# Unnormed rows from transposed loads, with the reciprocal rms applied where projections are evacuated

## The chip, the core and the metric

The kernel runs on one core of a Trainium2 chip. Its engines work side by side, each in the order of its own queue: TensorE (PE, with its weight loads as PEld), VectorE (DVE), ScalarE (ACT), GpSimd (POOL), and SyncE (SP), which here issues every DMA. The metric is device time in microseconds, the median of the runs.

## What is computed

One layer of a streaming encoder: y = x + W_out [A | B | M]. Every row of x is divided by its rms and multiplied by a gain g, and one input projection of the result is cut into columns for three groups of heads: A, differential attention (4 heads, with q and k normed per head); B, an mLSTM (4 heads); M, cross-attention into 256 memory tokens, whose rows are normed and projected in the same way. There are 1024 prompt tokens and 8 x 16 decode tokens, which have caches of 1024 keys.

```python
def rms_norm(x, g):
    xf = x.astype(F32)
    y = xf * lax.rsqrt(jnp.mean(xf * xf, axis=-1, keepdims=True) + EPS)
    return (y * g.astype(F32)).astype(x.dtype)
...
h = rms_norm(x, g_norm)
z = jnp.einsum('bsd,de->bse', h, w_in)
qa, ka, va, ga, qb, kb, vb, ob, ib, fb, gb, qm, gm = split_cols(z)
qa = rms_norm(qa.reshape(B, S, H_A, 2, DK_A), g_qa)
```

The reciprocal rms is one number for a row. It can be taken out of the sum over d: z is that number times the projection of the unnormed row. In q and k, which are normed again, it cancels except in the eps.

## The kernel before

The tokens are 9 tiles of 128 rows: the decode tile DEC first, then the prompt tiles from last to first (`order`). A product of fp32 precision is made of three: each operand is split into a hi part (fp32r) and a lo remainder, and hi x hi, hi x lo and lo x hi are summed in PSUM. With 8 steps over d a projection of a tile onto 512 columns has 24 products of 128x512 (`project`, L247). `weights` (L213) loads 8 tiles of a weight (`wraw`), makes the hi part `wh` on ACT (L231, the gain as scale) and the lo part `wl` on DVE (L238), or on POOL for the steps that a table names (L235 and L236; in phase A0 step 5).

The phases follow each other: A0 to A3 (the four heads of A; A0 also makes the transposed tiles `hth` and `htl` that all phases use), with the memory tiles between A0 and A1; then G (gates), M, B0 and B1 (pairs of heads of B, and beside them the decode attention over the caches, which loads 32 MB of keys and values), and the output projection O0 and O1. In phase A0 `norm_x` prepares a tile ahead of the one that is projected:

- The first tile (`norm_first`, L264) and the second (`norm_T` with `split_T`, L298 and L193) are squared on ACT for their sum, rooted on POOL (`root`, L133, as a power), scaled on DVE, transposed by PE (L279, L200), and split: the hi part copied on ACT, the lo part subtracted on DVE.
- Tiles 2 to 8 are loaded twice, as rows and, from a transposed input `xT`, already transposed. The rows serve only for the sum of squares (L287). PE then broadcasts the reciprocal rms over the partitions (a product of `xss` with the identity, L292), DVE scales `xT` by it (L294), ACT copies the hi part (L295), and DVE and POOL subtract a half each (L296).
- The two memory tiles are loaded as rows, scaled and transposed like the second tile, 8 transposes each.

Behind a projection come its stages. `a_post` squares q and k (ACT, L341), sums (DVE, L343), roots (POOL, L133, tile `asm`), multiplies (DVE, L345 and the gains in L395), transposes by PE (L404, tile `and__`) and splits again. The gate (`agt`) and the values (`avg`) are read from the same bank of PSUM, and the bank is free when they are. `PHASES` names the banks that z may use: in A0 two ("z").

Nothing orders the engines by hand: a scheduler lays out every engine's queue from the code and a few priorities. A change in one phase can therefore move instructions in all later ones.

Of the kernel before, what the change touches and what calls it, by code (L numbers as in the profile page):

```python
# [53 lines left out]
# steps of the decode attention after each tile of the head pairs of B  # L54
# [4 lines left out]
def hymba_step(ctx: ExitStack, tc: tile.TileContext, a: dict, o: dict):  # L59
# [61 lines left out]
    # ------------------------------------------------------------------ constants  # L121
# [39 lines left out]
    def small_loads():  # L161
# [3 lines left out]
        # carried here: the roots of n, the halves of silu and sigmoid (written with tanh), and, in  # L165
        # the gain of q, 8 * 0.125 / slope of the next head
# [20 lines left out]
        # sgn[r] = 1 on the rows of map 0, -lam on those of map 1, rows (h, m, q)  # L187
# [6 lines left out]
    def split_T(src, hi, lo, n):  # L194
        """transpose n [128,128] column blocks of src, split into hi and lo [128, n, 128]"""
# [7 lines left out]
    # the tensor engine's clock rises while the first loads run  # L203
# [9 lines left out]
    def weights(w, c0, n, gain=None, spare=()):  # L213
        """columns c0 to c0 + n of a [1024, .] weight, as hi and lo k-tiles; gain scales its rows.
        spare: (pool, tag, bufs) for raw tiles, where there is room"""
        wraw = (wpool, "wraw", 4)
        with ahead(phase.weights):
            src = [wraw] * 4 + [(p_, g_, b_) for p_, g_, b_ in spare for _ in range(b_)]
            ws = []
            for k in range(NK):  # L220
                p_, g_, b_ = src[k] if k < len(src) else wraw
                raw = p_.tile([P, 512], F32, tag=g_, name="wraw", bufs=b_)
                if spare and k == 6:
                    load_x(1)
                SY.dma_start(out=raw[:, 0:n], in_=w[k * P:(k + 1) * P, c0:c0 + n])
# [38 lines left out]
    def norm_first(xt, xp, hi, lo):  # L264
        ss = xp.tile([P, 3], F32, tag="xss0", name="xss0")
        for c in range(2):
            cs = slice(c * 512, c * 512 + 512)
            S.activation(flat(hi)[:, cs], xt[:, cs], AF.Square, accum_out=ss[:, c:c + 1])
        V.scalar_tensor_tensor(ss[:, 0:1], ss[:, 0:1], D * EPS, ss[:, 1:2], ALU.add, ALU.add)
        root(ss[:, 2:3], ss[:, 0:1])  # L270
        for c in range(4):
            cs = slice(c * 256, c * 256 + 256)
            V.tensor_scalar(xt[:, cs], xt[:, cs], ss[:, 2:3], math.sqrt(D), ALU.mult, ALU.mult)
            if c % 2:
                ks = slice(c * 2 - 2, c * 2 + 2)
                tv = bank("tp").rearrange("p (a b) -> p a b", b=P)
                for j in range(4):
                    x0 = (c - 1) * 256 + j * P
                    PE.transpose(tv[:, j, :], xt[:, x0:x0 + P], ident)  # L279
                S.copy(hi[:, ks], tv)  # L280
                V.tensor_tensor(lo[:, ks], tv, f(hi[:, ks]), ALU.subtract)  # L281

    def norm_T(xt, xp, hi, lo, xT=None):
        """rms-normed rows (gain not yet applied), transposed and split"""
        ss = xp.tile([P, 2], F32, tag="xss", name="xss", bufs=2)
        with ahead(50 if phase is PHASES["A0"] else 0):
            S.activation(hi.rearrange("p k d -> p (k d)"), xt, AF.Square, accum_out=ss[:, 0:1])  # L287
        rsqrt(ss[:, 1:2], ss[:, 0:1], D)
        if xT is not None:
            rb = bank("tp")[:, 0:P]  # L290
            mm(rb, ss[:, 1:2].broadcast_to([P, P]), ident)
            for c in range(0, NK, 4):  # L292
                cs = slice(c, c + 4)
# [389 lines left out]
    xts, xTs = {}, {}  # L683

    def load_x(i):
        if i < NT:
            xts[i] = shp.tile([P, D], F32, tag="usx", name="xt", bufs=4)
            if i == 0:
                for c in range(2):
# [617 lines left out]
```

## Time and profile before

| what | value |
| --- | --- |
| time, median of 3 runs | 783.51 us (783.5 to 788.57) |
| profiled execution, first to last instruction | 774.3 us |
| PE busy | 738.2 us (95%), 4976 products and transposes |
| DVE busy | 473.7 us (61%) |
| ACT busy | 333.4 us (43%) |
| POOL busy | 237.4 us (31%) |
| DMA | 106.19 MB, 44.2% of 16 engines' span |

The profile is of one execution. Its span runs from the first to the last instruction; of its time outside of the span only the difference to the runs is known, 9.2 us to the median. A busy share is a mean over the phases, so it is read together with the windows and with what each engine waited for. Products are pipelined and their ends are modelled, so the distance from one start to the next tells more than a duration.

### The profile page before, as it was taken

To read this page: it belongs to the slowest core of one execution; us is meant where nothing else is said; L and a number is where in the kernel's file an instruction comes from. 1 tells how busy PE (TensorE), PEld (TensorE's weight loads), DVE (VectorE), ACT (ScalarE), POOL (GpSimd) and SP (SyncE) were. 2 spreads that over 40 slices of the span, in tenths; PEclk is the share of its full clock that TensorE was granted. 3 is DMA by queue.
4 is the path that set the end of the run, shared out by engine and by line. 5 is a ranking of instruction groups with operands and counts; after the bars stand their busy time and mean duration, and the time that the engine had idled before them with its cause. 6 is when DMAs were issued, how large, how long until landed. Compare 5 with 4: busy or idle time off the path is not lost.

```text
span 774.3 us, 14523 instructions
## 1 busy us (share of the span) xinstructions
PE 738.2 (95%) x4976; PEld 599.9 (77%) x4976; DVE 473.7 (61%) x1466; ACT 333.4 (43%) x976; POOL 237.4 (31%) x332
## 2 busy tenths in 40 slices
PE   7998999999999999999999999899979997799998
PEld 6776788878888888998878776577747775578887
DVE  6788886677787778677575835347335347644111
ACT  6566634564664466555356532234223334200200
POOL 6653441323223223336313502111012036221500
PEclk9999999999999999999999999999989999999999
DMA  8733430151014112324002407979994728874422
GB/s 310 287 107 109 149 89 22 41 157 45 25 49 124 46 35 70 106 76 124 25 15 46 123 14 251 200 276 327 348 207 157 286 42 299 194 260 124 142 83 95
DMA packets 84387, 106.19 MB, mean 137 GB/s; under 512 B 16054, under 2 KB 52698, under 8 KB 84314
## 3 DMA queue, kind: packets, MB, share of 16 engines
q1 hardware_dynamic: 84314, 105.28, 44.2%
q8 instruction: 39, 0.64, 0.3%
q14 instruction: 34, 0.28, 0.1%
HBM read 86.01 MB, written 19.23 MB: 136 GB/s over the span
## 4 chain that ended last, share of the span: by engine, by line
PE 75%; DMA 9%; DVE 9%; issue 2%; ACT 2%; POOL 2%; SPq 0%; POOLq 0%; DVEq 0%; ACTq 0%
PE ps_z L95 39%; PE ps_y L95 15%; PE ps_s L95 9%; PE ps_av L95 5%; DMA kc<-in_kT_dram 4%; PE ps_tp L459 2%; DVE wl L238 2%; DMA mkc<-in_mkT_dram 1%; DMA wraw<-in_w_in_dram 1%; DMA bgt<-gated 1%; PE ps_tp L200 1%; PE ps_tp L867 1%; PE ps_tp L404 1%; DVE xT L294 1%; POOL asm L133 1%
## 5 line engine op out<-in xcount | busy, mean ns | idle before, releaser
L95 PE MATMUL ps_z<-wh,htl 128*128 128x512 f32 (+2 forms) x552 | 214.8, 391 | 0.1
L95 PE MATMUL ps_z<-wh,hth 128*128 128x512 f32 (+2 forms) x552 | 200.2, 394 | 4.4 <-ACT hth L280 2.1
L95 PE MATMUL ps_z<-wl,hth 128*128 128x512 f32 (+2 forms) x552 | 192.1, 387 | 0.0
L95 PEld LDWEIGHTS ps_z<-wh,hth 128*128 128x128 f32 x552 | 103.6, 190 | 25.5 <-ACT hth L280 2.4
L95 PEld LDWEIGHTS ps_z<-wh,htl 128*128 128x128 f32 x552 | 104.7, 190 | 18.9 <-DVE htl L281 0.8
L95 PEld LDWEIGHTS ps_z<-wl,hth 128*128 128x128 f32 x552 | 103.1, 189 | 18.6 <-issue 1.2
L95 PE MATMUL ps_y<-wh,htl 128*128 128x512 f32 (+2 forms) x176 | 65.6, 374 | 0.0
L95 PE MATMUL ps_y<-wh,hth 128*128 128x512 f32 (+2 forms) x176 | 62.9, 378 | 0.3 <-ACT oa L892 0.3
L133 POOL TENSOR_TENSOR asm<-asm,nhalf 128x4 f32<-128x4 f32 x36 | 39.6, 1100 | 74.4 <-DVE asm L137 58.8
L443 ACT ACTIVATE usx<-usx,usm 128x1024 f32<-128x1024 f32 (+7 forms) x64 | 49.7, 778 | 29.0 <-DVE usm L437 26.5
L95 PE MATMUL ps_y<-wl,hth 128*128 128x512 f32 (+2 forms) x176 | 61.3, 378 | 0.0
L238 DVE SCALAR_TENSOR_TENSOR wl<-wraw,gnm,wh 128x512 fp32r<-128x512 f32 (+1 forms) x62 | 47.0, 783 | 4.6 <-ACT wh L231 3.2
L231 ACT ACTIVATE wh<-wraw,gnm 128x512 fp32r<-128x512 f32 (+1 forms) x56 | 38.0, 706 | 18.2 <-DMA wraw<-in_w_in_dram 15.7
L95 PE MATMUL ps_s<-aqk 128*128 128x256 f32 (+1 forms) x160 | 42.0, 288 | 0.9 <-ACT aqk L412 0.9
L437 DVE CUSTOM_DVE_ANT_0 usx<-ps_s,tab 128x512 f32<-128x512 f32 (+3 forms) x64 | 37.0, 587 | 8.9 <-PE ps_s L95 7.5
L133 POOL TENSOR_TENSOR usm<-usm,nhalf 128x1 f32<-128x1 f32 x32 | 19.6, 612 | 72.3 <-DVE usm L467 67.9
L95 PE MATMUL ps_s<-akl,aqk 128*128 128x256 f32 (+1 forms) x160 | 41.0, 283 | 0.0
L95 PE MATMUL ps_av<-avg,wth 128*128 128x128 f32 x288 | 38.7, 276 | 0.2 <-DVE uot L469 0.2
L95 PEld LDWEIGHTS ps_av<-avg,wth 128*128 128x128 f32 x288 | 36.9, 191 | 2.5 <-ACT wth L460 0.6
L95 PEld LDWEIGHTS ps_y<-wh,hth 128*128 128x128 f32 x176 | 32.8, 188 | 5.8 <-ACT oa L892 0.6
L95 PEld LDWEIGHTS ps_y<-wl,hth 128*128 128x128 f32 x176 | 32.9, 188 | 5.5 <-DVE wl L238 0.3
L95 PEld LDWEIGHTS ps_y<-wh,htl 128*128 128x128 f32 x176 | 33.1, 188 | 5.0
(443 smaller groups left out, 1376.7 us busy)
## 6 DMA issues: line engine op xcount, KB each, us to landing
kc<-in_kT_dram SPq DMA_DIRECT2D x32, 512.0 KB, 8.9
vc<-in_cache_attn_v_dram SPq DMA_DIRECT2D x32, 512.0 KB, 6.8
wraw<-in_w_in_dram SPq DMA_DIRECT2D x56, 256.0 KB, 3.0
omx<-mixd SPq DMA_DIRECT2D x9, 512.0 KB, 4.1
out_dram<-oxt SPq DMA_DIRECT2D x17, 256.0 KB, 4.3
xt<-in_x_prompt_dram SPq DMA_DIRECT2D x8, 512.0 KB, 7.7
wraw<-in_w_out_dram SPq DMA_DIRECT2D x16, 256.0 KB, 4.2
oxt<-in_x_prompt_dram SPq DMA_DIRECT2D x16, 256.0 KB, 3.4
```

The source lines that it names most:

```text
L95: PE.matmul(out, lhsT, rhs, start=start, stop=stop)
L133: G.tensor_tensor(dst, ss, nhalf[:, 0:ss.shape[1]], ALU.pow)
L200: PE.transpose(tv[:, i, :], src[:, (c + i) * P:(c + i + 1) * P], ident)
L231: S.activation(wh[:, 0:n], raw[:, 0:n], AF.Copy, scale=g_)
L238: V.scalar_tensor_tensor(wl[:, 0:n], raw[:, 0:n], g_, f(wh[:, 0:n]), ALU.mult, ALU.subtract)
L294: V.scalar_tensor_tensor(xT[:, cs], xT[:, cs], math.sqrt(D), rep(rb, 4), ALU.mult, ALU.mult)
L404: PE.transpose(tp[:, i], flat(nd[:, 2 * i:2 * i + 2]), ident)
L437: V.tensor_tensor_reduce(s_[:, c * 512:c * 512 + w], sp[:, 0:w], tab[:, tx:tx + w], -slope, BIG if c == 0 else sm[:, m:m + 1], ALU.add, AL ...
L443: S.activation(s_[:, 0:nk], s_[:, 0:nk], AF.Exp, bias=last, scale=-1.0, accum_out=sm[:, 4 + m:5 + m])
L459: PE.transpose(tp[:, i], sx[0][:, (c + i) * P:(c + i + 1) * P], ident)
L867: PE.transpose(tp[0:pn, c - c0, :], se[:, c * P:c * P + pn], ident)
```

## The change

- x enters the projections unnormed. All nine tiles come from `xT`, the first in four pieces; `split_x` copies the hi part on ACT and subtracts the lo part, alternately on DVE and POOL. `norm_first`, `norm_T`, their transposes, scalings and broadcasts are gone. The memory has a transposed input too (`memT`).
- Rows are still loaded, for `row_stats`: the sum of squares (ACT), then mean plus eps and 64 eps times that (two DVE instructions of one column), the root (POOL), and the root's half and eighth (two POOL instructions of one column). They are kept in `rs`, one column for a tile.
- At every evacuation the reciprocal rms stands in: as the scale of a copy or a tanh instead of a constant or none; as a factor of an instruction that was there; or, in the gates of the decode tile and in phase G, as an added POOL multiplication. The eps of the second norms are scaled to match.
- In A0 z may use three banks ("zzy"). The loads are reordered: rows of the first tile after three weights, xT of the second and third tile before weight 6. `load_x(3)` is reached twice, from the prologue and from `norm_x(1)`.

```diff
-    "A0": Phase(300, 0, 0, 0, 4, "z", "SS", (5,), "S"),
+    "A0": Phase(300, 0, 0, 0, 4, "zzy", "SS", (5,), "S"),
...
-    def rsqrt(dst, ss, n):
-        V.tensor_scalar(ss, ss, n * EPS, None, ALU.add)
+    def rsqrt(dst, ss, n, t=None):
+        V.tensor_scalar(ss, ss, n * EPS if t is None else rsc(3, t), None, ALU.add)
         root(dst, ss)
+    def rsc(i, t):
+        return rs[:, i, t:t + 1]
...
+                if spare and k == 3:
+                    load_rows(0)
                 if spare and k == 6:
                     load_x(1)
+                    load_x(2)
...
+    def row_stats(rows, t, xp):
+        ss = xp.tile([P, 2], F32, tag="xss", name="xss", bufs=2)
+        for i, x in enumerate(rows):
+            S.activation(x, x, AF.Square, accum_out=ss[:, i:i + 1])
+        if len(rows) > 1:
+            V.tensor_tensor(ss[:, 0:1], ss[:, 0:1], ss[:, 1:2], ALU.add)
+        V.tensor_scalar(rsc(4, t), ss[:, 0:1], 1.0 / D, EPS, ALU.mult, ALU.add)
+        V.tensor_scalar(rsc(3, t), rsc(4, t), 64.0 * EPS, None, ALU.mult)
+        root(rsc(0, t), rsc(4, t))
+        G.tensor_scalar(rsc(1, t), rsc(0, t), 0.5, None, ALU.mult)
+        G.tensor_scalar(rsc(2, t), rsc(0, t), 0.125, None, ALU.mult)
+
+    def split_x(xT, hi, lo, n=2):
+        for i in range(n):
+            ks = slice(i * NK // n, (i + 1) * NK // n)
+            S.copy(hi[:, ks], xT[:, ks])
+            (V, G)[i % 2].tensor_tensor(lo[:, ks], xT[:, ks], f(hi[:, ks]), ALU.subtract)
...
-        S.activation(gt, z[:, 384:512], AF.Tanh, scale=0.5)
+        S.activation(gt, z[:, 384:512], AF.Tanh, scale=rsc(1, t))
...
+        if t == DEC:
+            G.tensor_scalar(gt, gt, rsc(0, t), None, ALU.mult)
...
-        S.copy(vg[:, j], z[:, 256:384])
+        S.activation(vg[:, j], z[:, 256:384], AF.Copy, scale=rsc(0, t))
...
+            t = order[i]
+            split_x(xTs.pop(i), hth[t], htl[t], 4 if i == 0 else 2)
+            load_x(i + 4 if i % 2 == 0 else i + 2)
...
-            norm_T(flat(mxt), ap, *mhl[t])
+            split_x(mxt, *mhl[t])
             if t == 0:
                 load_mem(1)
+            mem_stats(t)
...
             small_loads()
+            load_x(3)
             with ahead(200):
                 norm_x(0)
+            row_stats([xts.pop(0)], order[0], ap)
         for i, t in enumerate(order):
             if h == 0:
                 norm_x(i + 1)
+                if i:
+                    row_stats([xts.pop(i)], t, ap)
+                load_rows(i + 1)
...
             th4 = heads(th, 4)
+            G.tensor_scalar(th, th, rsc(0, t), None, ALU.mult)
             G.tensor_tensor(th4, th4, rep(gmh, 4), ALU.mult)
```

The scheduler's order shows three places. The first is PE's queue at the end of the first tile's products. Before, `hth_127` is the decode tile and `hth_126` the second one:

```order
L95 MATMUL ps_z<-wh,hth_127 128x512
L95 MATMUL ps_z<-wl,hth_127 128x512
L95 MATMUL ps_z<-wh,htl_136 128x512
L200 MATMUL ps_tp<-ident,xt 128x128 x8
L95 MATMUL ps_z<-wh,hth_126 128x512 x8
L95 MATMUL ps_tp<-ident,xss 128x128
```

In the change `hth_128` is the decode tile, `hth_127` and `hth_126` the second and third:

```order
L95 MATMUL ps_z<-wh,hth_128 128x512
L95 MATMUL ps_z<-wh,hth_127 128x512 x6
L95 MATMUL ps_y<-wh,hth_126 128x512 x6
L95 MATMUL ps_z<-wl,hth_128 128x512
L95 MATMUL ps_z<-wh,htl_137 128x512
L95 MATMUL ps_z<-wh,hth_128 128x512
L95 MATMUL ps_z<-wh,hth_127 128x512
L95 MATMUL ps_y<-wh,hth_126 128x512
```

The first tile is no longer finished before the second begins: after the hi product of step 5 come six hi products of each of the next two tiles, and only then the product with the lo part of step 5 (`wl`). The transposes are gone.

The second place is POOL's queue at the same time. Before:

```order
L133 TENSOR_TENSOR xss_231<-xss_231,nhalf 128x1
L387 MEMSET akl 64x256
L388 MEMSET akl 64x256
L235 TENSOR_SCALAR wraw<-wraw,gnm 128x512
L387 MEMSET akl 64x256
L388 MEMSET akl 64x256
L236 TENSOR_TENSOR wl<-wraw,wh 128x512
```

And in the change, where L245 and L246 are the weight's lines and L293 is the lo half of `split_x`:

```order
L133 TENSOR_TENSOR rs<-rs,nhalf 128x1
L285 TENSOR_SCALAR rs<-rs 128x1
L286 TENSOR_SCALAR rs<-rs 128x1
L245 TENSOR_SCALAR wraw<-wraw,gnm 128x512
L384 MEMSET akl 64x256
L385 MEMSET akl 64x256
L293 TENSOR_TENSOR htl_136<-xT,hth_127 128x512
L246 TENSOR_TENSOR wl<-wraw,wh 128x512
```

The weight's lo part, the product's operand of step 5, now stands behind the row statistics of the first tile and behind a lo half of the second.

The third place is PE's queue around the transposes of q and k (L404 before, L401 in the change) of the second tile, `and__427` before and `and__406` in the change. Before, with `hth_125` the third tile and `hth_124` the fourth:

```order
L95 MATMUL ps_z<-wl,hth_125 128x512
L404 MATMUL ps_tp<-ident,and__427 128x128 x2
L95 MATMUL ps_tp<-ident,xss 128x128
L95 MATMUL ps_z<-wh,hth_124 128x512 x8
L95 MATMUL ps_z<-wh,htl_133 128x512
```

In the change `hth_125` is the fourth tile:

```order
L95 MATMUL ps_z<-wh,htl_134 128x512
L401 MATMUL ps_tp<-ident,and__406 128x128 x2
L95 MATMUL ps_z<-wl,hth_125 128x512
L95 MATMUL ps_z<-wh,htl_134 128x512
L95 MATMUL ps_z<-wl,hth_125 128x512
L95 MATMUL ps_z<-wh,hth_124 128x512 x8
```

The transposes moved from the end of the next tile's products into those of the tile after it, and no broadcast of `xss` stands between them and the products that follow.

## Rows read from the trace of the kernel before

**Rows 1.** The page's part 1: busy us (share of the span), instructions.
```profile
PE 738.2 (95%) x4976; PEld 599.9 (77%) x4976; DVE 473.7 (61%) x1466; ACT 333.4 (43%) x976; POOL 237.4 (31%) x332
```

**Rows 2.** Windows: busy us (instructions) by engine; PE clock, DMA share, GB/s.
```profile
40.00:60.00 20.00, 17.27 (x81) 13.61 (x80) 16.77 (x39) 11.81 (x32) 10.81 (x12) 1.00 0.36 104
...
100.00:120.00 20.00, 20.00 (x106) 16.98 (x105) 15.94 (x50) 8.67 (x25) 6.04 (x10) 1.00 0.22 64
```

**Rows 3.** Timeline, PE, 0-20 us: start, duration, line, tiles, count, [idle <- releaser].
```profile
2.29 5.33 PE L95 MATMUL ps_tp<-ident 128*128 128x128 f32 x24 [2.29 <-POOL ident masks.py:199]
...
10.73 0.80 PE L95 MATMUL ps_z<-wh,hth 128*128 128x512 f32 x1 [2.13 <-ACT hth L280]
...
15.20 0.40 PE L95 MATMUL ps_z<-wh,htl 128*128 128x512 f32 x1
...
18.17 1.03 PE L200 MATMUL ps_tp<-ident,xt 128*128 128x128 f32 x8
19.50 0.73 PE L95 MATMUL ps_z<-wh,hth 128*128 128x512 f32 x2 [0.29 <-ACT hth L78]
```

**Rows 4.** Waits of PE, 10 to 95 us: total us, times, longest.
```profile
PE ps_tp L404 <- DVE and__706 L395: 1.3, 1, 1.3
PE ps_z L95 <- ACT mht L78: 1.1, 1, 1.1
PE ps_s L95 <- ACT aqk L412: 0.9, 1, 0.9
...
PE ps_tp L200 <- DVE mht L192: 0.5, 1, 0.5
```

**Rows 5.** Timeline of tiles of A0, several engines.
```profile
36.89 0.42 DVE L395 TENSOR_TENSOR and__496<-asq,vecs 128x256 f32<-128x256 f32 x1
...
50.04 1.28 POOL L296 TENSOR_TENSOR htl<-xT,hth 128x512 fp32r<-128x512 f32 x1
50.05 1.55 DVE L395 TENSOR_TENSOR and__636<-asq,vecs 128x256 f32<-128x256 f32 x1
...
51.75 0.41 PE L404 MATMUL ps_tp<-ident,and__636 128*128 128x128 f32 x2 [0.71 <-DVE and__636 L395]
51.99 0.39 PE L95 MATMUL ps_tp<-ident,xss 128*128 128x128 f32 x2
52.14 2.10 PE L95 MATMUL ps_z<-wh,hth 128*128 128x512 f32 x8
```

**Rows 6.** Timeline of PE: first products of A0's fourth tile; A0's end.
```profile
32.56 2.10 PE L95 MATMUL ps_z<-wh,hth 128*128 128x512 f32 x8
...
71.14 0.38 PE L404 MATMUL ps_tp<-ident,and__829 128*128 128x128 f32 x2
```

**Rows 7.** By line, 10-100 us: count | busy us, mean ns | idle.
```profile
L133 POOL TENSOR_TENSOR asm<-asm,nhalf 128x4 f32<-128x4 f32 x9 | 11.1, 1231 | 14.0 <-DVE xss L137 8.8 <-DVE asm L137 5.0
...
L294 DVE SCALAR_TENSOR_TENSOR xT<-xT,ps_tp 128x512 f32<-128x512 f32 x14 | 9.4, 684 | 2.6 <-PE ps_tp L95 2.5
L296 POOL TENSOR_TENSOR htl<-xT,hth 128x512 fp32r<-128x512 f32 x7 | 9.0, 1284 | 0.0
...
L133 POOL TENSOR_TENSOR xss<-xss,nhalf 128x1 f32<-128x1 f32 x10 | 6.0, 600 | 1.8 <-DVE xss L137 1.8
```

**Rows 8.** Timeline of ACT and POOL at the start: the weights' split.
```profile
6.02 4.18 ACT L231 ACTIVATE wh<-wraw,gnm 128x512 fp32r<-128x512 f32 x6 [1.09 <-DMA wraw<-in_w_in_dram]
...
10.38 2.40 POOL L235 TENSOR_SCALAR wraw<-wraw,gnm 128x512 f32<-128x512 f32 x1 [2.94 <-ACT wh L231]
...
13.48 1.29 POOL L236 TENSOR_TENSOR wl<-wraw,wh 128x512 fp32r<-128x512 f32 x1
```

**Rows 9.** DMA rate, 0 to 100 us in 40 slices of 2.5 us.
```profile
GB/s 75 277 353 368 410 419 339 262 409 413 396 319 52 159 340 55 203 36 92 170 28 209 61 35 44 0 79 0 157 277 269 265 242 7 105 0 190 234 100 208
```

**Rows 10.** PE's waits, whole span; view of tile th (min/median/max ns).
```profile
PE ps_s L95 <- DMA kc<-in_kT_dram: 7.0, 3, 3.2
...
L791 POOL TENSOR_TENSOR th<-th,vecs x9: 733/746/763, 314.8 to 352.6; 128x256 f32<-128x256 f32 x9
```

More of the change, by code (lines that the diff above doesn't have):

```diff
@@ L151, in hymba_step @@
     gif = cpool.tile([P, 2, NT, 4], F32, name="gif")
+    rs = cpool.tile([P, 5, NT + 2], F32, name="rs")
     aN, gwN, wsN, emN = (nat[:, i] for i in range(4))
@@ L262, in project @@
         return z
[L264 to L281, printed above, removed]
@@ L283, in norm_T @@
-    def norm_T(xt, xp, hi, lo, xT=None):
-        ss = xp.tile([P, 2], F32, tag="xss", name="xss", bufs=2)
[L286 to L293, printed above, removed]
-                V.scalar_tensor_tensor(xT[:, cs], xT[:, cs], math.sqrt(D), rep(rb, 4), ALU.mult, ALU.mult)
-                S.copy(hi[:, cs], xT[:, cs])
-                (V, G)[c // 4].tensor_tensor(lo[:, cs], xT[:, cs], f(hi[:, cs]), ALU.subtract)
-            return
-        V.tensor_scalar(xt, xt, ss[:, 1:2], math.sqrt(D), ALU.mult, ALU.mult)
-        split_T(xt, hi, lo, NK)
+    def row_stats(rows, t, xp):
+        ss = xp.tile([P, 2], F32, tag="xss", name="xss", bufs=2)
+        for i, x in enumerate(rows):
[7 more added lines that the diff above has]
+        G.tensor_scalar(rsc(2, t), rsc(0, t), 0.125, None, ALU.mult)
@@ L355, in a_post_dec @@
     def a_post_dec(h, z):
-        sq = a_norm(z)
+        sq = a_norm(z, DEC)
         vo = ap.tile([P, P], F32, tag="pp", name="avd", bufs=4)
-        S.copy(vo, z[:, 256:384])
+        S.activation(vo, z[:, 256:384], AF.Copy, scale=rsc(0, DEC))
         hc = slice(h * P, (h + 1) * P)
@@ L466, in a_unit @@
         S.activation(ot, av, AF.Square, accum_out=sm[:, 9:10])
[L467 removed]
+        V.scalar_tensor_tensor(sm[:, 9:10], sm[:, 9:10], sm[:, 6:7], rsc(4, t), ALU.add, ALU.mult)
         root(sm[:, 10:11], sm[:, 9:10])
@@ L590, in mem_q @@
         V.tensor_reduce(sm[:, 0], sq, AX.X, ALU.add)
-        rsqrt(sm[:, 2], sm[:, 0], 64)
-        S.activation(gt, z[:, 256:512], AF.Tanh, scale=0.5)
+        rsqrt(sm[:, 2], sm[:, 0], 64, t)
+        S.activation(gt, z[:, 256:512], AF.Tanh, scale=rsc(1, t))
         V.scalar_tensor_tensor(gt, gt, 1.0, z[:, 256:512], ALU.add, ALU.mult)
@@ L686, in load_x, with load_rows @@
         if i < NT:
-            xts[i] = shp.tile([P, D], F32, tag="usx", name="xt", bufs=4)
-            if i == 0:
-                for c in range(2):
-                    cs = slice(c * 512, c * 512 + 512)
-                    SY.dma_start(out=xts[i][:, cs], in_=xsrc(order[i], cs))
-                return
+            if i % 2:
+                xTs[i] = shp.tile([P, NK, P], F32, tag="usx", name="xT", bufs=4)
+            else:
+                xTs[i] = mp.tile([P, NK, P], F32, tag="mk", name="xT", bufs=2)
+            n = 4 if i == 0 else 1
+            for c in range(n):
+                ks = slice(c * NK // n, (c + 1) * NK // n)
+                SY.dma_start(out=xTs[i][:, ks], in_=a["xT"][order[i]][:, ks])
+    def load_rows(i):
+        if i < NT:
+            xts[i] = shp.tile([P, D], F32, tag="usx", name="xt", bufs=4)
             SY.dma_start(out=xts[i], in_=xsrc(order[i]))
-            if i >= 2:
-                xTs[i] = mp.tile([P, NK, P], F32, tag="mk", name="xT", bufs=2)
-                SY.dma_start(out=xTs[i], in_=a["xT"][order[i]])
     def norm_x(i):
         if i < NT:
-            load_x(i + 3)
-            hi, lo = hth[order[i]], htl[order[i]]
-            if i:
-                norm_T(xts.pop(i), ap, hi, lo, xTs.get(i))
-            else:
-                norm_first(xts.pop(i), ap, hi, lo)
+            t = order[i]
+            split_x(xTs.pop(i), hth[t], htl[t], 4 if i == 0 else 2)
+            load_x(i + 4 if i % 2 == 0 else i + 2)
     def mem_stages(t):
@@ L736, in load_mem, with mem_stats @@
     def load_mem(t):
-        SY.dma_start(out=flat(mxt), in_=a["mem_prompt"][0, t * P:(t + 1) * P, :])
+        SY.dma_start(out=mxt, in_=a["memT"][t])
+    def mem_stats(t):
+        rows = []
+        for c in range(2):
+            x = shp.tile([P, 512], F32, tag="wth", name="mrow", bufs=3)
+            SY.dma_start(out=x, in_=a["mem_prompt"][0, t * P:(t + 1) * P, c * 512:(c + 1) * 512])
+            rows.append(x)
+        row_stats(rows, NT + t, ap)
     def mem_chunk():
@@ L992, in mlstm_in @@
         th = bw.tile([P, P], F32, tag="bth", name="bth", bufs=2)
-        S.activation(th, z[:, 384:512], AF.Tanh, scale=0.5)
+        S.activation(th, z[:, 384:512], AF.Tanh, scale=rsc(1, t))
         V.scalar_tensor_tensor(gt, th, 1.0, gt, ALU.add, ALU.mult)
```

34 lines of the change are left out of this document (16 added, 18 removed).

## The prediction

> **What bounds the kernel now.** I read the busy times first. TensorE (PE) is busy 738.2 of 774.3 us [rows 1]: little is to be won except where it waits or does work that can go. The windows of 20 us then say where that is. From 100 us on PE is full in most of them (20.00 of 20), but between 40 and 60 us it has 17.27 while VectorE (DVE) has 16.77 [rows 2]. That is phase A0, in which x is normed, transposed and projected for the first time, and this is where the change works. The timeline of PE's start shows a warm-up until 7.62 (2.29 + 5.33), the first product at 10.73 after 2.13 of waiting for the normed and transposed tile, products 0.228 apart from 15.20 on (13 of them to 18.17), then 8 transposes in 1.03 for the second tile, whose products start at 19.50 [rows 3]. PE's waits from 10 to 95 us name the rest [rows 4]: transposes of q and k (L404) that wait for DVE's multiply L395 (1.3 once, and 0.7 three times, as in [rows 5]), and, around the memory tiles, 1.1, 0.9 and 0.5.
>
> The timeline of one tile shows why [rows 5]. PE's queue holds L404, behind it the broadcast of the next tile's rms (ps_tp<-ident,xss), behind that the next products. L404 stands at 51.75 because L395 on DVE took 1.55 there, begun within 0.01 us of a 1.28 us subtraction on POOL; where POOL is quiet the same instruction takes 0.42. Only the broadcast lets DVE scale the next xT. So every tile goes once round PE, DVE, ACT and back.
>
> The sum is made against the profiled execution: span 774.3. The median of the three runs is 783.51, 9.2 more, which lies outside the first and last instruction; I leave it as it is and subtract the gain from 783.5.
>
> **The change, term 1: the start of A0.** Removed are the first tile's square, root, scaling and 8 transposes, and the second tile's scaling and 8 transposes. Added is a wait for transposed tiles and a longer load queue: 4 xT pieces, 3 weights, the sample's rows, 3 weights, three xT tiles, and only then weights 6 and 7. I replay it (durations under 1.3 us without a row are rounded from this stretch). By the DMA rate in slices of 2.5 us [rows 9], 0.19, 0.88, 1.76, 2.68, 3.71, 4.75, 5.60 MB have come after each slice. Before, 0.79 MB stood up to the first weight, 4.7 us by that sum, and ACT began on it at 6.02 [rows 8]; I add 1.0 to 1.3 us to each landing.
> - Weight 0 has the same bytes ahead and a few more issues: 6.4, its hi part by 7.1 (0.7 each on ACT, 4.18 for 6). PE's warm-up ends 7.62; three k-steps run to about 9.7, paced by the weights.
> - The rows (0.52 MB) stand before weight 3: ACT squares them about 9.0 to 10.3, weight 3 is split by 11.7, weight 4 by 12.4. The 15 products of k0 to k4 are through at 13.1.
> - The second tile's xT ends at 3.15 MB, 12.1 us, the third's at 13.4; ACT copies each in halves of 0.6. 13 hi products (one of tile 0, 6 each of the next two) fill PE from 13.1 to about 16.1.
> - Then PE wants the lo part of weight 5, which POOL makes. POOL first takes the root for the rows (inputs at 10.6, about 1 us), two tiny scalings, the weight's scaling (2.40), memsets 0.6, the second tile's lo half (1.28) and then the subtraction (1.29) [rows 7, 8]: 17.9. PE waits some 1.8.
> With 28 products done at 17.9, 44 more of 0.228 complete three tiles at 27.9; two transposes are 0.2, and the fourth tile waits some 0.8 more for the bank of the first, whose gate ACT reads only after squaring the third. It starts at 29.1 where it now starts at 32.56 [rows 6]. **Term 1: 3.5 us.** Bounds: without both waits 2.6 more. If each tiny scaling costs as much as the root (0.6, same shape and engine [rows 7]) instead of my 0.2, and the root as much as the wider one (1.23), the start is 1.0 later; a DMA lag 1 us larger makes it 2.1 later. Between 1.4 and 6.1.
>
> **Term 2: the other six tiles of A0.** From 32.56 to 71.1 [rows 6] are six tiles, 6.43 each. Removed per tile: the broadcast, 0.15 on PE (51.99 to the next product at 52.14), the scaling of xT on DVE (two of 0.684 [rows 7]), and the ring. The L404 waits of these six are 0.7, 0.7 and 1.3 [rows 4, 5]; they go because the transposes of a tile now stand in the products of the second tile behind it and a third bank holds z. **Term 2: 2.7 + 6 x 0.15 = 3.6 us**, 5.83 a tile. What must hide below that: DVE runs at 16.77/20 of 6.43 = 5.4 a tile, less 1.37, plus two small ones of 0.15, is 4.3. POOL per tile: asm root 1.23, lo half 1.28, row root 0.6, two tiny ones (0 to 0.6 each, 0.2 taken here as well), the gate's multiply (at most 0.75, the row of a double width [rows 10]): 4.3. ACT trades squares and copies for equal ones. Both fit, but POOL more tightly. Bounds: 0 (below) to 3.6.
>
> [...] The row: L395 with POOL's 1.28 us subtraction beside it takes 1.55, alone 0.42 [rows 5]. [...]
>
> **Term 3: the memory tiles.** 16 transposes go; 8 take 1.03 [rows 3], so 2.0. Of the waits 1.1 + 0.9 + 0.5 [rows 4] those for transposed halves go; PE still follows the new weights, split at 0.7 to 0.8 on ACT and DVE against 0.68 for three products, so I keep 1.0 and take 1.5. The second memory tile has its load earlier, as nothing on PE reads its buffer. **Term 3: 3.5 us**, between 2.0 and 4.5.
>
> **Term 4: scalings at other evacuations.** Copies that became scaled copies, constants that became columns, and an add that became a fused one cost nothing on paths shown; they are hidden behind PE at 20 of 20 [rows 2]. Phase G adds one POOL scaling of 128x256 per tile, near L791's 0.75, nine of them [rows 10]: 6.7 if the cover, POOL's waiting there, is gone. PE does not wait for POOL's gate; only the last, at 352.6, stands close to the next weights. **Term 4: -0.6**, between 0 and -6.7. The decode tile's extra scalings (one for each head and one in M) sit on the same idle engine.
>
> **DMA.** Two more xT tiles, the memory rows, and one load that is issued twice (i = 3, from the prologue and from tile 1): 2.5 x 1.05 MB, 6.6 us at 400 GB/s. They lie in the first 35 us; after that the rates are 0 to 277 [rows 9], and the tiles needed then have landed. What each load is late for is in term 1.
>
> **Later phases.** The scheduler orders all that follows anew. Instruction counts there are equal, and PE is the chain, so the gain is carried through; but where PE waits for keys (7.0 in 3 waits [rows 10]) the order of loads shifts by a place here and there. I add 0, and plus or minus 4.
>
> Sum: 3.5 + 3.6 + 3.5 - 0.6 = 10.0. Span 764.3, time **773.5**.
>
> **Rivals.**
> 1. [...] 0.20.
> 2. *The later phases give it back.* Two or three more waits for keys of 3.2, the longest now [rows 10]: 8 lost, 781.5. For: loads in that stretch do change places. Against: those waits follow the loads' own chain, which starts earlier with all else. 0.12.
> 3. *Slower: POOL becomes the bound of A0.* [...] It decides from 6.43 + 7/8 = 7.3 a tile. Against: at 40 to 60 us POOL is at 10.81 of 20 [rows 2]. 0.05.
> 4. *More*: no wait at the start and an order that helps later, 766. 0.05.
>
> **Numbers.** The forecast holds 0.58, as 769.5 to 777.5 by its own terms. Faster by over 1% (below 775.7; about what a measurement of this kernel can tell from no change) takes 0.8 of it, 0.3 of rival 1 and all of 4: 0.57. Slower by over 1% is rival 3: 0.05. The rest, 0.38, is within 1%. The range from 767.5 to 781.5 leaves out rival 3, part of 2 and part of 4.
>
> **What would show it.** The first product between 7 and 8 us; a PE wait for weight 5's lo part near 16 to 18; the first product of tile 3 near 29 and A0's last near 64; no wait on q and k transposes; no PE broadcast; POOL about 4.3 us a tile. Wrong if tiles of A0 take over 6.2, if the fourth tile starts after 31, or if PE's waits after 450 us grow by more than 4.

## The result

The change takes 796.99 us (median; 795.55 to 799.1) against 783.5 of the kernel before beside it: a ratio of 1.0158, with a 95% interval of 1.0123 to 1.0192. It is slower, where 773.5 (767.5 to 781.5) was forecast. The profiled execution took 797.59 and spans 795.8 us; the one of before spans 774.3. The page's part 1 answers to [rows 1]; under it stands the granted clock of PE in 40 slices of the span, first of the change, then of before.

```profile
PE 747.0 (94%) x4930; PEld 600.8 (75%) x4930; DVE 467.9 (59%) x1455; ACT 347.9 (44%) x980; POOL 256.5 (32%) x373
...
PEclk9999999999999999999999999899989998989999
```
```profile
PEclk9999999999999999999999999999989999999999
```

PE has 46 instructions less and is busy 8.8 us longer, because it is slowed more often: four slices of the change are below 0.9 of full speed, one of before. The mean granted clock is 0.974 against 0.989. PE's idle time (span less busy) is 48.8 against 36.1. The two together are nearly the whole difference of 21.5 us: idle time grew by 12.7; the time lost to the clock, (1 - clock) x span, is 20.7 against 8.5, so 12.2 more; the removed work takes some 3 off. All profiles below add up like this: span less idle less clock loss is between 718 and 734.

Where it is lost is read from the start times of the same work in the two traces. In the last four rows PE has issued the same instructions up to there, but for the 46 that are removed and at most seven others:

| first instruction of PE, us | before | change | lead |
|---|---|---|---|
| fourth tile of A0 | 32.56 | 32.91 | -0.4 |
| first memory tile | 73.02 | 67.16 | +5.9 |
| transposes of attention weights (A1) | 115.28 | 109.05 | +6.2 |
| first transposes of the memory queries (M) | 374.54 | 374.67 | -0.1 |
| first scores of the decode attention | 476.56 | 487.00 | -10.4 |
| first scores of the memory decode | 653.49 | 674.95 | -21.5 |

So A0 is faster, and the later phases lose 28 us: 6.3 from A1 to M's first queries (2.9 of it behind 336 us), 10.3 in the 112 us from there to the decode attention, and 11.1 up to the memory decode. PE's waits from 360 to 480 us, first of the change, then of before (total us, times, longest):

```profile
PE ps_z L95 <- DVE mgt L590: 3.3, 2, 2.6
PE ps_tp L652 <- ACT gT L646: 3.0, 2, 2.5
PE ps_z L95 <- DVE msq L598: 1.7, 1, 1.7
PE ps_s L95 <- DVE mqs L620: 0.5, 2, 0.4
```
```profile
PE ps_s L95 <- DMA kc<-in_kT_dram: 1.1, 1, 1.1
PE ps_tp L646 <- DVE mgt L642: 0.5, 1, 0.5
PE ps_z L95 <- DVE mgt L593: 0.4, 1, 0.4
```

A projection waits for a bank that the memory gate (`mgt`) still has to leave. This wait costs twice: behind its 2.6 us, which end at 380.97, PE is granted 0.66 in a window of 5 us (clock and DMA share are the third- and second-last columns); in windows of 0.5 us it is 0.50 from 381.5 to 384.5 and 1.00 from 380 to 381 and from 385 to 390. Not every wait does: the 1.7 us one for `msq`, which ends at 368.36, is followed by 1.00 until 375.

```profile
375.00:380.00 5.00, 3.01 (x19) 2.19 (x17) 4.22 (x14) 2.87 (x10) 2.88 (x12) 1.00 0.19 54
380.00:385.00 5.00, 4.03 (x11) 3.17 (x12) 4.75 (x18) 2.66 (x9) 1.70 (x9) 0.66 0.00 0
```

Behind M, PE's waits for keys, which answer to [rows 10], have grown by 4.9 over the whole span, and the wait for `mb`, a tile of phase B that took 2.2 before, takes 6.4:

```profile
PE ps_s L95 <- DMA kc<-in_kT_dram: 11.9, 5, 5.8
PE ps_s L95 <- DVE mb L1025: 6.4, 1, 6.4
```

### The profile page after: what moved, and what is told of

Read it like the earlier page. It is cut to its first block, busy times and chain, and to the rows that moved or that the text cites. A ratio compares the mean times of both kernels' runs of the same rounds, so it can differ in the third digit from the quotient of the medians.

```text
span 795.8 us, 14505 instructions
## 1 busy us (share of the span) xinstructions
PE 747.0 (94%) x4930; PEld 600.8 (75%) x4930; DVE 467.9 (59%) x1455; ACT 347.9 (44%) x980; POOL 256.5 (32%) x373
## 4 chain that ended last, share of the span: by engine, by line
PE 68%; DMA 10%; DVE 6%; issue 3%; ACT 2%; POOL 1%; SPq 0%; DVEq 0%; POOLq 0%; ACTq 0%
PE ps_z L95 36%; PE ps_y L95 13%; PE ps_s L95 9%; DMA kc<-in_kT_dram 6%; PE ps_av L95 5%; DVE wl L248 1%; DMA wraw<-in_w_in_dram 1%; PE ps_tp L456 1%; DMA mvc<-in_cache_mem_v_dram 1%; DMA mixd<-oa 1%; PE ps_tp L877 1%; PE ps_tp L207 1%; PE ps_tp L652 1%; DVE usx L434 1%; DMA mb<-mtd 1%
## 5 line engine op out<-in xcount | busy, mean ns | idle before, releaser
L95 PE MATMUL ps_z<-wh,htl 128*128 128x512 f32 (+2 forms) x528 | 207.3, 393 | 0.0
L95 PE MATMUL ps_z<-wh,hth 128*128 128x512 f32 (+2 forms) x528 | 196.0, 398 | 8.2 <-DVE mgt L590 3.3
L95 PE MATMUL ps_z<-wl,hth 128*128 128x512 f32 (+2 forms) x528 | 185.7, 391 | 2.2 <-POOL wl L246 1.8
L95 PEld LDWEIGHTS ps_z<-wl,hth 128*128 128x128 f32 x528 | 99.4, 190 | 20.7 <-POOL wl L246 2.2
L95 PE MATMUL ps_y<-wh,htl 128*128 128x512 f32 (+2 forms) x200 | 75.7, 380 | 0.0
L95 PE MATMUL ps_y<-wh,hth 128*128 128x512 f32 (+2 forms) x200 | 70.1, 386 | 2.3 <-DVE agt L345 1.1
L95 PE MATMUL ps_y<-wl,hth 128*128 128x512 f32 (+2 forms) x200 | 70.8, 380 | 0.0
L440 ACT ACTIVATE usx<-usx,usm 128x1024 f32<-128x1024 f32 (+7 forms) x64 | 49.7, 777 | 46.1 <-DVE usm L434 44.4
L95 PEld LDWEIGHTS ps_y<-wh,hth 128*128 128x128 f32 x200 | 37.7, 191 | 10.3 <-ACT wh L241 2.0
L95 PEld LDWEIGHTS ps_y<-wh,htl 128*128 128x128 f32 x200 | 38.0, 190 | 6.0
L95 PEld LDWEIGHTS ps_y<-wl,hth 128*128 128x128 f32 x200 | 37.5, 188 | 5.9
```

Source lines behind the costliest of these rows:

```text
L95: PE.matmul(out, lhsT, rhs, start=start, stop=stop)
L440: S.activation(s_[:, 0:nk], s_[:, 0:nk], AF.Exp, bias=last, scale=-1.0, accum_out=sm[:, 4 + m:5 + m])
```

## The experiments

Three theories stood at first. **Order**: the scheduler lays out all later queues anew, and the new order is worse. **Price**: column scales on ACT and the added multiplications on POOL cost where they stand. **A0**: the new start is what costs the time. Times are ratios to runs of the kernel before on the same chip, since that kernel's own median was between 777.3 and 783.5 from one comparison to the next.

| run | ratio (95%) | PE idle, us | clock |
|---|---|---|---|
| the change | 1.0158 (1.0123 to 1.0192) | 48.8 | 0.974 |
| A0 alone | 1.0001 (0.9969 to 1.0033) | 41.0 | 0.985 |
| evacuations alone | 1.0380 (1.0322 to 1.0438) | 57.9 | 0.975 |
| change, one tag of banks | 1.0384 (1.0319 to 1.0448) | 59.8 | 0.966 |
| before, one column | 1.0309 (1.0260 to 1.0358) | 53.0 | 0.980 |
| before, scales of M | 1.0129 (1.0098 to 1.0160) | 42.0 | 0.976 |
| change, M with three banks | 1.0249 (1.0208 to 1.0290) | 57.4 | 0.968 |
| change, pool off | 1.0159 (1.0117 to 1.0202) | 50.4 | 0.978 |
| before, M with three banks | 1.0152 (1.0105 to 1.0199) | 52.2 | 0.976 |
| change in old order | 1.0046 (1.0026 to 1.0066) | 39.4 | 0.980 |
| before in new order | 1.0265 (1.0227 to 1.0303) | 50.8 | 0.979 |
| pool off in old order | 1.0031 (1.0008 to 1.0053) | 38.2 | 0.987 |
| gate in the root | 1.0021 (0.9993 to 1.0049) | 39.6 | 0.986 |
| keys earlier | 1.0065 (1.0036 to 1.0094) | 44.4 | 0.978 |

### The parts apart

```diff
-        S.activation(gt, z[:, 384:512], AF.Tanh, scale=rsc(1, t))
+        S.activation(gt, z[:, 384:512], AF.Tanh, scale=0.5)
...
-            G.tensor_scalar(th, th, rsc(0, t), None, ALU.mult)
```

> The change's A0 and memory phase (unnormed transposed loads, statistics on the side, three banks), but every evacuation of a projection takes the constants of the kernel before in place of a row's reciprocal rms; the rows are therefore not normed in the output. From phase G on the instructions of TensorE and VectorE stand in exactly the order of the kernel before. Order theory (the loss comes from the order into which the scaled evacuations throw the later phases): the 3.6 us by which the change led at the gate rows are carried to the end, so 3 to 8 below the kernel before, 776 to 781. Price theory (a column scale on ScalarE and the added multiplications on GpSimd cost where they stand): the same 776 to 781, as both are gone. A0 theory (the new start, its loads and its clock cost the time): as slow as the change, 793 or more.

Measured 1.0001: no loss, and no gain. Counted by equal work, it leads before by 6.7 from 150 to 205 us and by 3.0 from 215 on. The difference goes around one wait, of 1.41, behind which the window from 205 to 210 is granted 0.70. From G on every instruction of PE stands where it did: the lead stays 3.0 to 480 us, falls by 7.4 in the decode attention, to -4.4 at 640, and is -2.7 at the end. PE's wait at 204.69, then those for keys (7.0 in before):

```profile
204.69 1.11 PE L454 MATMUL ps_tp<-ident,usx 128*128 128x128 f32 x4 [1.41 <-DVE usx L446]
...
PE ps_s L95 <- DMA kc<-in_kT_dram: 13.5, 6, 5.6
PE ps_s L95 <- DMA mkc<-in_mkT_dram: 3.7, 1, 3.7
```

The A0 theory falls: the new start alone does not make the kernel slower. The lead is real, and is given back.

```diff
+    for i_, v_ in enumerate((1.0, 0.5, 0.125, 64.0 * EPS, 1.0)):
+        G.memset(rs[:, i_], v_)
...
-        S.activation(gt, z[:, 384:512], AF.Tanh, scale=0.5)
+        S.activation(gt, z[:, 384:512], AF.Tanh, scale=rsc(1, t))
```

> The kernel before with the change's evacuations only: columns that hold 1, 0.5, 0.125, 64 eps and 1 stand where the change has a row's values, and the added multiplications are there. Order theory: 6 to 18 slower than the kernel before, 789 to 801, and the loss lies in waits of TensorE for z banks in phase M and for keys in the decode attention, which stand at other places. Price theory: slower too, by the sum of the added durations on the path, 2 to 10 (785 to 793), spread evenly over G, M and B. A0 theory: within 3 of the kernel before.

Measured 1.0380, or 29.5 us, where the prices were to make 2 to 10. Only 3.5 us are lost up to the first memory tile (76.48 against 73.02).

```diff
-    "A0": Phase(300, 0, 0, 0, 4, "zzy", "SS", (5,), "S"),
+    "A0": Phase(300, 0, 0, 0, 4, "z", "SS", (5,), "S"),
```

> The change with two banks for the projections of A0 (z only) as before. From G on TensorE's order is that of the run with the evacuations alone. Order theory: the time of that run less the lead of A0 (about 3), and up to 4 more in A0 for waits on banks, so within 4 of that run, whatever the change itself takes. Price theory: the change's time plus 0 to 4 (797 to 801). A0 theory: as the change, 794 to 801.

Measured 1.0384, the time of the run above and 2.2% more than the change. It decides nothing: its first memory product is at 76.73, where the change has 67.16, so 9.6 of the 15.2 us between the two spans (811.0 and 795.8) are lost in A0 itself, at waits that two banks bring:

```profile
PE ps_tp L367 <- DVE asq L361: 6.4, 1, 6.4
```

Nor is its later order quite that of the run above: the traces agree in 0.94 of PE's places from G on, and in all of them only from some 376 us on.

```diff
-        V.tensor_scalar(ss, ss, n * EPS, None, ALU.add)
+        V.tensor_scalar(ss, ss, n * EPS if n != 64 else e64, None, ALU.add)
```

> The kernel before with one edit: the small constant that is added before the root of q's and k's rms comes from a column that holds it. It touches 128x4 instructions on VectorE alone (0.17 us, perhaps 0.05 more each, some 50 of them, none of which TensorE waits for by the rows), but the scheduler lays the later phases in another order (TensorE's agrees with that of the kernel before in 0.80 of its places). Order theory: it moves by several us, to either side, 775 to 800, with waits of TensorE at other places. Price theory and A0 theory: within 2 of the kernel before.

Measured 1.0309, 24 us, beyond what I had expected. By line, the instructions that the edit touches (first this run, then before: count | busy us, mean ns):

```profile
L137 DVE TENSOR_SCALAR asm<-asm,e 128x4 f32<-128x4 f32 x36 | 8.2, 228 | 0.8
L137 DVE TENSOR_SCALAR msm<-msm,e 128x4 f32<-128x4 f32 x11 | 2.8, 250 | 0.3
```
```profile
L137 DVE TENSOR_SCALAR asm<-asm 128x4 f32<-128x4 f32 x36 | 6.3, 175 | 0.9
L137 DVE TENSOR_SCALAR msm<-msm 128x4 f32<-128x4 f32 x11 | 2.1, 190 | 0.1
```

The price is 11.0 - 8.4 = 2.6 us on an engine that is idle for 40% of the span. The other 21 cannot be it, and what else changed is the order; for this run itself the orders were not exchanged.

### Price or banks in M

```diff
-        S.activation(gt, z[:, 256:512], AF.Tanh, scale=0.5)
+        S.activation(gt, z[:, 256:512], AF.Tanh, scale=rsc(1, t))
...
-        V.tensor_scalar(sm[:, 1], sm[:, 1], 0.5, None, ALU.mult)
+        V.tensor_scalar(sm[:, 1], sm[:, 1], rsc(1, t), None, ALU.mult)
```

> The kernel before with the change's evacuations in phase M alone (the tanh of the memory gate and the factor of its softmax sum take a column that holds 0.5; two lesser edits, the scaled copy of the memory values and the fused add of the gates in G, and the decode tile's gate multiplication with a column of ones, come with it). TensorE's order agrees with that of the kernel before in 0.95 of all places, VectorE's in 0.93. Price theory: M, where the change loses 14 us against the kernel before, is where these prices lie, so 5 to 14 slower, 782 to 791. Order theory: nearly the same order, so nearly the same time: within 4 of the kernel before, and no wait of TensorE for the memory gate above 1 us.

Measured 1.0129, within the price theory's range; but the loss is not where the price is. PE's wait for the memory gate, 360 to 480 us, is 0.6 once:

```profile
PE ps_z L95 <- DVE mgt L602: 0.6, 1, 0.6
```

From the first transposes of the memory queries to the last products of the memory attention it takes 94.2 us, where before takes 92.1 and the change 103.0. It loses 4.4 up to 115 us, where its edits are one multiplication for the decode tile and two scaled copies, and some 10 behind the first scores of the decode attention, where it has none. So the price theory loses its place. The order theory's forecast, within 4 us, failed too: an order that agrees in 0.95 of its places is no guard against 1.3%.

```diff
-    "M": Phase(200, 100, 0, 4, 3, "z", "SS", (2, 4, 6), "S"),
+    "M": Phase(200, 100, 0, 4, 3, "zzy", "SS", (2, 4, 6), "S"),
```

> The change with three banks in turn for the projections of phase M instead of two. If the loss in M is TensorE standing for a bank (2.6 for the memory gate at 381, 1.7 for the square at 368, and the halved clock behind them), those waits go and the kernel reaches the first score of the decode attention 6 to 12 us earlier than the change (487.0 in its profile: 475 to 481). The time as a whole by the order theory: anything from 780 to 805, since the order behind M is thrown anew (0.78 of places as in the change). By the price theory: the change's time less 0 to 8, 788 to 797.

> The kernel before with three banks for phase M instead of two: no instruction is added, removed or made longer, and a wait for a bank can only go. TensorE's order agrees with that of the kernel before in 0.83 of its places. Order theory: the time moves by several us to the slow side, as with the small constant from a column, 785 to 805, because the order of the kernel before is better than most. If a bank is what M lacks: 772 to 778. Price theory: within 2 of the kernel before, 775 to 779.

The second is the same edit in the kernel before. Measured 1.0249 and 1.0152: a bank more, no work more, and the kernel before becomes slower than with two. In the change the wait of 2.6 for the gate's bank is gone, but one of 8.9 has come at the gate's transposes; in the kernel before, the same place goes from 0.5 to 7.6. PE's waits, 360 to 490 us, of the two runs:

```profile
PE ps_tp L644 <- DVE mgt L640: 8.9, 1, 8.9
```
```profile
PE ps_tp L646 <- DVE mgt L642: 7.6, 1, 7.6
```

The change with three banks reaches the first scores at 489.17, not at 475 to 481. A bank is not what M lacks.

### The start

```diff
-    "A0": Phase(300, 0, 0, 0, 4, "zzy", "SS", (5,), "S"),
+    "A0": Phase(300, 0, 0, 0, 4, "zzy", "SS", (), "S"),
```

> The change with the lo part of A0's weight 5 made by VectorE instead of GpSimd. It tests the start. If the stand of 1.8 us that ends at 19.20, and the halved clock behind it, are what kept the fourth tile at 32.91 instead of the forecast 29.1, then no wait for a GpSimd weight is left, the clock stays at full after 13 us, and the fourth tile's first product stands at 28.5 to 30. If VectorE is as late with that part, or the clock falls at the start whatever is waited for, it stays within 1 of 32.9. The time as a whole by the order theory: 780 to 805, whatever the start gains; by the A0 theory the change's time less 3 to 4, 793.

The fourth tile now starts at 29.80 (timeline of PE). But a window behind the 1.38 us stand is granted 0.66, and at the memory tiles 1.4 of the 3.1 us are left. The run below that joins this start to the old order has the same stand, of 1.38, and is granted 1.00 behind it; its memory tiles start 2.8 ahead of the change (64.35). The whole time of pool off is the change's.

```profile
28.99 0.44 PE L367 MATMUL ps_tp<-ident,asq 128*128 128x128 f32 x2 [1.38 <-DVE asq L361]
29.80 3.44 PE L95 MATMUL ps_z<-wh,hth 128*128 128x512 f32 x8 [0.38 <-DVE agt L345]
```
```profile
25.00:30.00 5.00, 3.25 (x15) 2.27 (x14) 3.84 (x15) 1.83 (x7) 3.55 (x7) 1.00 1.04 403
30.00:35.00 5.00, 5.00 (x16) 3.96 (x16) 3.60 (x10) 3.97 (x9) 4.48 (x8) 0.66 0.99 380
```

What had kept the fourth tile is POOL's queue. Behind weight 5 POOL works without a break up to the roots of q and k (`asm`), which begin at 29.97. DVE, which prepares them, has itself stood 2.96 for a product of POOL's (`lamv`) that is queued behind weight 5 too. PE's transposes of q and k (L367) need the roots, and stand ahead of the fourth tile in PE's queue. Without weight 5's two instructions on POOL (1.59 and 1.71) the roots begin 3.0 earlier. POOL and DVE in the change, then POOL in pool off:

```profile
17.43 1.71 POOL L246 TENSOR_TENSOR wl<-wraw,wh 128x512 fp32r<-128x512 f32 x1
...
27.22 0.29 DVE L181 TENSOR_REDUCE cst<-lamv 128x2 f32<-128x128 f32 x1 [2.96 <-POOL lamv L180]
...
29.37 0.58 POOL L133 TENSOR_TENSOR rs<-rs,nhalf 128x1 f32<-128x1 f32 x1
29.97 2.00 POOL L133 TENSOR_TENSOR asm<-asm,nhalf 128x4 f32<-128x4 f32 x2
```
```profile
26.98 2.03 POOL L133 TENSOR_TENSOR asm<-asm,nhalf 128x4 f32<-128x4 f32 x2
```

The clock at the start is not what kept it: the run "gate in the root", below, has the change's order in A0 and a granted clock of 1.00 from 10 to 30 us, and its fourth tile starts at 33.05.

### The orders exchanged

The order itself can be prescribed: a table of instruction names for each engine, and for each neighbouring pair an edge that fixes only which is issued first.

```diff
+        for a, b in zip(names, names[1:]):
+            tc.add_manual_dep(byname[b], a, info, reason="order")
```

> The change, every instruction of it, with one thing prescribed: from A1's first weight on, each engine (TensorE, VectorE, ScalarE, SyncE, and GpSimd but for its 13 added multiplications, which the scheduler places) issues its instructions in the order of the kernel before. Only issue order is prescribed; no wait is added between engines. Order theory: the loss goes, and the lead of A0 (6.2 us at the first attention transposes in the change's profile) is carried at least in part: 0.990 to 1.000 of the kernel before. Price theory (the scaled evacuations cost what they cost wherever they stand): 1.008 to 1.018, near the change's own 1.0158. Both in part: between.

> The converse: the kernel before, unchanged in every instruction, but from A1's first weight on in the order in which the change's instructions stand. No column scale, no added multiplication, A0 as before. Order theory: it is as slow as the change or slower, by the lead that A0 lacks: 1.015 to 1.030 of the kernel before. Price theory: within 0.3% of the kernel before.

Measured 1.0046 and 1.0265. This settles it: with the old order the change loses only 0.5% instead of 1.6%, and with the new order the untouched kernel becomes slower than the change. The untouched kernel then also shows the change's waits in M, with none of its added work; in the change with the old order the wait for the gate's bank is down to 0.4. PE's waits from 360 us on, before in new order, then change in old order:

```profile
PE ps_z L95 <- DVE mgt L593: 3.3, 2, 2.5
PE ps_tp L654 <- ACT gT L648: 2.2, 2, 1.7
PE ps_z L95 <- DVE msq L600: 1.6, 1, 1.6
```
```profile
PE ps_z L95 <- DVE mgt L590: 0.4, 1, 0.4
```

The edges alone, on the kernel before in its own order, were not run; but three runs that have them (this one and two below) come within 0.2 to 0.5% of before.

Where the remaining 0.46% goes can be followed, since PE's instructions correspond one to one from A1 on. The lead is 7.0 at the memory tiles, 3.7 from 90 to 160 us, 1.2 at 345, -1.4 at 350, and -4.2 at the end. Only the step in phase G, at 345 to 350, was traced to a cause. Timeline of POOL, DVE and PE there, change in old order, then before:

```profile
342.20 2.74 POOL L800 TENSOR_SCALAR th<-th,rs 128x256 f32<-128x256 f32 x3 [2.60 <-DVE th L798]
...
344.91 2.12 POOL L801 TENSOR_TENSOR th<-th,vecs 128x256 f32<-128x256 f32 x3
...
346.98 0.58 POOL L133 TENSOR_TENSOR usm<-usm,nhalf 128x1 f32<-128x1 f32 x1
...
347.59 0.35 DVE L466 SCALAR_TENSOR_TENSOR uot<-ps_av,usm,ugt 128x128 f32<-128x128 f32 x1 [2.41 <-POOL usm L133]
...
348.00 1.38 PE L95 MATMUL ps_av<-avg,wth 128*128 128x128 f32 x10 [1.36 <-DVE uot L466]
```
```profile
343.34 2.15 POOL L791 TENSOR_TENSOR th<-th,vecs 128x256 f32<-128x256 f32 x3 [2.58 <-DVE th L789]
...
345.66 0.98 POOL L133 TENSOR_TENSOR usm<-usm,nhalf 128x1 f32<-128x1 f32 x1 [0.16 <-DVE usm L467]
...
346.68 0.35 DVE L469 SCALAR_TENSOR_TENSOR uot<-ps_av,usm,ugt 128x128 f32<-128x128 f32 x1 [0.36 <-POOL usm L133]
```

Three added multiplications (2.74) stand ahead of a small root. Behind the root DVE reads the bank `ps_av`, and PE waits 1.36 for that, where before it did not wait. By 360 us this step has cost 2.0.

Pool off and the old order together:

> The change with A0's weight 5 made by VectorE alone and, from A1's first weight on, the order of the kernel before. Its start was 3.1 us earlier at the fourth tile and 2.2 earlier at the first attention transposes than the change's (106.84 against 109.05). Order theory: 0 to 3 us below the change in the old order, 0.987 to 0.998 of the kernel before, and the fastest of all so far. Price theory: 1.005 to 1.016. If the later phases take back any lead (waits for keys whose loads do not come earlier): no different from the change in the old order.

Measured 1.0031: its median is 0.7 us below that of the change in the old order, and the two intervals overlap. Of the start's gain little arrives.

```diff
-            G.tensor_scalar(th, th, rsc(0, t), None, ALU.mult)
...
+        V.tensor_scalar(sm[:, 2], sm[:, 2], rsc(4, t), None, ALU.mult)
         root(sm[:, 3], sm[:, 2])
```

> The change with two things altered. The nine multiplications of 128x256 by a column on GpSimd in phase G go: the row's reciprocal rms of that gate is taken in later, by a 128x2 multiplication on VectorE ahead of the root of the head norm. And from A1's first weight on the issue order is that of the run with A0 alone (constants at the evacuations), which on TensorE and VectorE is that of the kernel before from G on. If GpSimd's gate multiplications in G are the price that the change in the old order pays (2.5 us lost between 340 and 352, where the root behind three of them ends TensorE's wait), that loss is gone: the lead at the transposes of the gates, -0.9 there, is 1.5 to 3.5, and the time is 0.997 to 1.001 of the kernel before, 2 to 4 us below the change in the old order. If the price lies elsewhere (column scales on ScalarE, wherever they stand): 1.003 to 1.007 as before, lead below 1.

Measured 1.0021, level with before, and G's step is gone: between 340 and 360 us the lead rises by 0.7, where in the change in the old order it falls by 2.0. The lead at the gates' transposes is 0.3, not the 1.5 to 3.5 expected; this execution led by only 4.4 at the memory tiles and lost some 2 more at 208 to 215 us. So what G costs is shown in the trace, not in the time: the run also changes the order of A1 to A3, and its interval overlaps that of the change in the old order.

One of the two places in SP's prescribed order:

```diff
+DMA kc[128, 1024]<-in_kT_dram@524288
 DMA out_11_dram[128, 8, 64]@0<-C
 DMA out_12_dram[128, 8, 1]@0<-C
-DMA kc[128, 1024]<-in_kT_dram@524288
```

> As the run with the gate in the root, and two of the 32 key loads of the decode attention are issued earlier on SyncE's queue: the one that stands behind two stores of the state C (some 3 us) and the one that stands behind four stores of the running state, for which SyncE stood 5.6 us. If the lead is lost in the decode attention because keys are issued behind stores that wait for other engines, TensorE's two long waits for keys (3.3 near 496 and 4.7 near 576 in the change in the old order) fall below 1.5 each and the time is 0.990 to 0.997 of the kernel before. If the loads are late by the rate of the transfers instead, the waits stay, or move to the next load, and the time is within 0.2% of the run with the gate in the root.

Measured 1.0065, 4.5 us more than the run with the gate in the root. The waits for keys fall from 9.4 (3 times) to 2.2, and others come up. PE's waits of this run, whole span:

```profile
PE ps_y L95 <- ACT ems L897: 9.0, 1, 9.0
PE ps_tp L1005 <- DVE ewt L80: 3.8, 1, 3.8
...
PE ps_s L95 <- DMA kc<-in_kT_dram: 2.2, 4, 1.1
```

So issue order was what kept those keys. That moving them is what delays the others is likely, but was not tested by itself. No version was clearly faster than before.

## Why the prediction was wrong

- **Later phases, "I add 0, and plus or minus 4": the step that failed.** I wrote that the scheduler orders all that follows anew, and costed it at nothing because PE is the chain and the instruction counts are equal. The runs show that the order alone is worth as much as all the terms that I summed, or twice as much: the old order takes 1.1% (9 us) off the change, and the new order adds 2.7% (21 us) to the untouched kernel. With equal counts PE waits at other places, and behind some waits it is granted a lower clock (the untouched kernel has a median of 0.981 over its runs in the new order and 0.985 in its own). A comparison of the two orders, which could have been made beforehand, finds PE's sequence from G on in agreement in only 0.75 of its places. Eight kernels whose later order the scheduler made otherwise, the change among them, are 1.3 to 3.8% slower than before; A0 alone, with the old order from G on, is level. Two of the signs that I named did show: the fourth tile started after 31, and PE's waits behind 450 us grew by 4.7 (18.7 to 23.4).
- **The base of the sum.** I subtracted from 783.5 and laid 9.2 us outside the span. In every later run the time is 1.8 us more than the span (777.0 and 778.84, A0 alone). So the profiled execution took some 776, and executions of one kernel differ by up to 1%: the sum mixed two of them. This is not what failed: from 776 the sum gives 766, further from the result.
- **Term 1, 3.5 forecast, -0.4 measured.** The wait for weight 5's lo part came as named and ended at 19.20, not 17.9. But the replay ended POOL's account there. It left out what still stands in its queue ahead of the roots of q and k: lo halves, five scalings of `vecs` (some 0.5 each), the product for `lamv` and the second tile's row root, until 29.97. PE was also granted 0.74 and 0.72 in the windows 10 to 15 and 20 to 25 us, but a run without that starts its fourth tile no earlier (33.05). Over the five kernels that share this order of A0 the term is -0.7 to +0.8; pool off, which takes weight 5 out of the queue, makes it 2.8.

```profile
19.20 0.64 PE L95 MATMUL ps_z<-wl,hth 128*128 128x512 f32 x1 [1.82 <-POOL wl L246]
...
31.97 0.44 PE L367 MATMUL ps_tp<-ident,asq 128*128 128x128 f32 x2 [0.90 <-DVE asq L361]
...
32.91 1.39 PE L95 MATMUL ps_z<-wh,hth 128*128 128x512 f32 x5 [0.51 <-DVE agt L345]
```

- **Term 2, 3.6 forecast, some 4.4 measured: right.** From 32.91 to the first memory product at 67.16 are six tiles of 5.71 (5.83 forecast). POOL has 4.8 a tile, not 4.3, and it still fits. The windows that answer to [rows 2] show PE full:

```profile
40.00:60.00 20.00, 20.00 (x93) 16.38 (x92) 15.25 (x50) 17.78 (x45) 16.80 (x32) 1.00 0.66 205
60.00:80.00 20.00, 20.00 (x91) 15.84 (x90) 16.87 (x45) 15.86 (x39) 7.72 (x12) 1.00 0.55 158
```

- **Term 3, 3.5 forecast, some 2 measured**, at its lower bound. From A0's end (71.36 before, 67.16 in the change) to A1 the lead grows from 4.2 to 6.2. 1.7 of it stand ahead of the first memory product, where the kernel before has transposes (0.60) and a wait (1.06). Terms 1 to 3 were to give 10.6 and gave 6.2; what is missing is term 1 and part of this one.
- **Term 4, -0.6 forecast, -2.0** at the one place traced, in the old order. I looked for PE waiting for POOL's gate; what PE waits for is a root behind it in POOL's queue. ACT's prices were real too: the copy of values took 0.369 with a column scale (L388) and 0.268 without (L391), and the gate's tanh 0.368 (L344) and 0.293 (L350): 101 and 75 ns more. With all of them in place, and only POOL's multiplications in G gone, the run "gate in the root" is level with before (1.0021), so in the old order they cost little.
- **Rivals.** The first (1, chance 0.20): no run shows the loss that it counted. DVE's lo half in A0 did rise from a mean of 683 ns (33 to 72 us in before, where POOL is busy for 19.31 of 39) to 957 (33 to 67 in the change, 28.09 of 34), but a tile took 5.71, no longer than the 5.83 forecast. POOL as A0's bound (3) did not come, though POOL had 16.80 of 20. Giving back (2) did come: 7.4 in the decode attention of the A0-alone run, at waits for keys. No rival was slower by way of the order, and that was the chance I should have made large.

## What to carry to other kernels

Where a scheduler lays out the queues, the order is part of the kernel, and an edit's price cannot be added up without it: compare the orders first, and where they differ, give the loss of the old order a term and a chance of its own. Here even 0.95 of places in agreement did not protect. To measure an edit, prescribe the old order and run the edit in it, and run the old kernel in the new order. A saving at the front of a chain is worth only what the next waits leave of it: with the old order, 7.0 us at the memory tiles were 1.2 at 345 us and none at the end.

## What was not expected of the hardware

A column in place of a constant on DVE instructions of 128x4 (0.05 us each, 2.6 in all) went with 24 us, by way of the order as far as is known. Some waits as short as 1.4 to 2.6 us were followed by windows of 5 us at 0.66 or 0.70 of the clock (2.6 in the change, 1.41 in A0 alone), while others as long were not: the same wait of 1.38, in the same start, was followed by 0.66 in one execution (pool off) and by 1.00 in another (pool off in old order). The waits were thus paid for again in PE's speed: in the profiled executions the clock takes 8.5 us in before and 20.7 in the change. What takes the lead in the decode attention is not settled: with earlier key loads the waits for keys went and others came.
